# Seven-product pairs in half of the first quarter of layer 0's w1, with the input differences made during w_out

## The chip, the cores and the metric

The kernel runs on one core of one Trainium2 chip. The metric is the device time of one execution in microseconds (us). An execution is one launch that computes both layers for one sequence of 528 positions (16 meta tokens and 512 tokens).

## The reference: what is computed

The reference is a decoder trunk of two layers, all in float32. The part that matters here is the channel mixer, which follows the token mixer in each layer:

```python
def sq_relu_mlp(h, w1, w2):
    return jnp.square(jax.nn.relu(h @ w1.astype(h.dtype))) @ w2.astype(h.dtype)
...
        h = h + mix                       # mix ends with "@ w_out" in layer 0
        h = h + sq_relu_mlp(rmsnorm(h, norm_mlp_g[layer]), mlp_w1[layer], mlp_w2[layer])
```

h has 528 rows of 1024, w1 is 1024 x 4096 and w2 is 4096 x 1024. The mixer of layer 0 ends with a product with w_out (2048 x 1024), whose result is added to h.

## The kernel before, in words

**Layout.** Activations lie transposed: 1024 features are eight tiles of 128 partitions, each with 528 columns (positions). h0 to h7 are the residual stream. Each float32 operand of a matmul is split in two parts, a rounded one (names that end in h or hi) and the rest (l or lo), and a product takes three matmuls: hi·xh, hi·xl and lo·xh. One matmul is 128 x 128 weights by 264 columns.

**A plain product** (`gemm`) makes one tile of 128 output features for all 528 columns: 8 input tiles x 3 terms x 2 halves = 48 matmuls into the PSUM tile `mm`, of which there are two in turn. `prepare` makes the weights two products ahead: the load `raw`, ScalarE's cast to `whi`, and the subtraction for `wlo`, which is done on GpSimd for w_in and w_out and on VectorE for w1 and w2. There are three `whi` and three `wlo` buffers.

**A pair** is two output tiles made together by seven products instead of eight (Strassen-Winograd): the weights of both tiles are halved by input features (two loads `pr` of 512 KB), and the columns are halved too. Each of the seven products, A11, A12, S2, S3, S1, A22 and S4, is 4 input tiles x 3 terms = 12 matmuls into a PSUM tile `pp`, of which there are four in turn. S1 to S4 are sums of weight quarters (L231, VectorE, tiles `S`). Their splits are a cast on ScalarE (L246) and a subtraction on VectorE (L247). Nearly every product is read from PSUM by VectorE (`add` in `product`, L1037), which forms the rows `r` from them; A11 is copied by ScalarE to `snap` (L1039). `finish` applies the relu and the norm (L1021), and `squares` makes the next operand (ScalarE twice, then VectorE, L979). The next pair's S1 needs that pair's second `pr`, whose buffer comes free when the last use of an earlier one is done; there are three.

**The input's differences** (`differences(k)`, k = 0 to 3) are the column-half combinations that S1, S2 and S3 multiply with: two scaled copies and three casts on ScalarE, and seven VectorE instructions (L955 to L958, three of L963). S4's operand is written over half of x by `difference4`, during the last plain product.

**Order of the work.** w_out is done in two parts of eight products each. In the second (`residual`), each product is added to h by VectorE (L491), split to `x1h` and `x1l` (L420, L421), and its square is summed on GpSimd (`n1s`, L435). Then the PSUM pools are closed and opened anew, so that the first product of w1 takes the bank of w_out's last and waits for the addition to h7. In the MLP, the first 1024 hidden features (the first quarter, c = 0) are made by eight plain products, whose results wait for the norm `m0rb`; the differences are made during products 1 to 4. Then quarters 1 to 3 are made by four pairs each, and between them (`back`, after every second unit of two products) come the eight plain products of w2 for the quarter before. Layer 1 does the same with 512 columns.

**What sets the order.** From w_out on, TensorE, VectorE, ScalarE and GpSimd run their instructions in the order in which the code issues them (`manual_schedule`), except for a short stretch at w1's start, which a scheduler orders. Each engine works in order. Loads are issued by SyncE's queue, in order; a load waits until its buffer is free.

Of the kernel before, what the change touches and what calls it, by code (L numbers as in the profile page):

```python
# [17 lines left out]
P = 128  # L18
SEQ = 512
NMETA = 16  # L20
T = SEQ + NMETA
HT = T // 2
D = 1024
NK = D // P
# [105 lines left out]
H = NK // 2  # L130


PRODUCTS = [(kind, i) for i in range(NPAIR) for kind in ("A11", "A12", "S2", "S3", "S1", "A22", "S4")]


def mlp_units(layer):

    units = [(f"w1_{layer}", 0, m * P) for m in range(NK)]
    for c in range(1, 4):
        w2 = [(f"w2_{layer}", (c - 1) * D, m * P) for m in range(NK)]  # L140
        for j in range(len(PRODUCTS) // 2):
            units.append((f"s_{layer}", c, j))
            if j % 2:
                units.append(w2.pop(0))
        units += w2
    return units + [(f"w2_{layer}", 3 * D, m * P) for m in range(NK)]


def blocks():

    out = []
    for name, r, c in unit_order():
        if name[:2] != "s_":
            out.append((name, r, c))
        elif c == 0:
            out += [(f"w1_{name[2:]}", 0, r * D + m * P) for m in range(NK)]
    return out


@with_exitstack  # L160
def trunk(ctx, tc, xT, wts, par, con, out):
# [7 lines left out]
    def psums(n):  # L169
        st = ExitStack()  # L170
        return (st, st.enter_context(tc.tile_pool(name="pmm", bufs=2, space=PSUM, reuse_waits="tile")),
                st.enter_context(tc.tile_pool(name="pax", bufs=n, space=PSUM, reuse_waits="tile")))

    psum, pmm, pax = psums(2)
# [31 lines left out]
    class Pairs:  # L206

        def __init__(self, layer, pl):
            self.layer, self.pl = layer, pl
            self.todo = [(c, m) for c in range(1, 4) for m in range(NK)]  # L210
            self.raw, self.sums, self.used = {}, {}, {}
            self.live = 0

# [50 lines left out]
    def piece():  # L264
        if pieces:
            pieces.pop(0)()
# [120 lines left out]
    def gemm(what, x, n, at=NK, each=None):  # L387

        w = weights(what)
        ps = pmm.tile([P, 2, 512], F32, tag="mm", name=f"mm{state['unit']}")  # L390
        width = HT if n == T else SEQ
        halves = [(slice(i * width, i * width + width), ps[:, i, :width]) for i in range(n // width)]
        for k in range(NK):
            if k == at:
                between.chain_up()
            products(halves, w, k, x[k], k == 0, k == NK - 1)
            if each:
                each(k)
            if k % 2:
                between.step()  # L400
                piece()
        return ps[:, :, :HT] if n == T else ps[:, 0, :SEQ]

    def v2(ap, n):
        return two(ap) if n == T else ap
# [49 lines left out]
    def square(src, n, name):  # L455
        sq = sp.tile([P, T], F32, tag="sq", name=name)
        nc.scalar.activation(sq[:, :n], src, AF.Square)
        return sq[:, :n]
# [24 lines left out]
            return rb, xv  # L483
        return rb

    def residual(what, x, n, norm=None, xset=None, name="", keep=True):

        s = Sum(name, n) if norm is not None else None
        for m in range(NK):
            ps = gemm(what, x, n)  # L490
            nc.vector.tensor_tensor(v2(h[m][:, :n], n), ps, v2(h[m][:, :n], n), ALU.add)  # L491
            if norm is not None:
                split_g(xset[m], h[m][:, :n], col(PC_NORM + norm * NK + m), n)
                s.add(square(h[m][:, :n], n, f"{name}q{m}"))
        return s


    poolA = ExitStack()
    actA = poolA.enter_context(tc.tile_pool(name="actA", bufs=1, reuse_waits="tile"))
# [10 lines left out]
    engines = {nc.tensor.engine, nc.vector.engine, nc.scalar.engine, nc.gpsimd.engine}  # L510
# [28 lines left out]
    s = Sum("n0", T, nc.vector)  # L539
# [374 lines left out]
    setC = free[1]  # L914

    setD = new_set(act, "B", "x1")
    s = residual("w_out", setC, T, 2, setD, "n1")
    manual.close()
    mix.close()

    NQ, MW = 4, 32


    def mlp(layer, x, s, n, mine, after):
        hw = n // 2
        first, second = slice(0, hw), slice(hw, n)
        g = lambda k: col(PC_NORM + (2 + layer) * NK + k)
        with tc.tile_pool(name=f"mlp{layer}", bufs=1, reuse_waits="tile") as pl:
            hid = {}
            work = Pairs(layer, pl)  # L930
# [35 lines left out]
            def difference4(k):  # L966

                hi, lo = (t[:, second] for t in x[k])
                nc.scalar.activation(hi, t4[k], AF.Copy, scale=-1.0)
                nc.vector.scalar_tensor_tensor(lo, t4[k], -1.0, hi.bitcast(F32), ALU.mult, ALU.subtract)  # L970
# [8 lines left out]
                return lambda: nc.vector.tensor_tensor(dst[1][:, :n], q, dst[0][:, :n].bitcast(F32), ALU.subtract)  # L979

            what = f"w1_{layer}"
            ps = gemm(what, x, n)
            rb = rstd(s, f"m{layer}")
            work.load()
            manual = ExitStack()
            for m in range(NK):
                if m:

                    ps = gemm(what, x, n, each=(lambda k: k < H or difference4(k - H)) if m == NK - 1 else None)
                if m in (1, 2, 3, 4):  # L990
                    differences(len(t4))
                r = row(f"0{m}")
                nc.vector.scalar_tensor_tensor(v2(r, n), ps, 0.0, v2(rb[:, :n], n), ALU.max, ALU.mult)
                squares(hidden(0, m), r, f"0{m}")()
                if m == 0:
                    manual.enter_context(tc.manual_schedule(engines=engines))
# [16 lines left out]
                    e[1]()  # L1013

            stt = nc.vector.scalar_tensor_tensor
            for c in range(1, 4):
                rows = {}

                def finish(i, e, op):
                    r = rows[e]  # L1020
                    stt(r, r, 0.0, rb[:, :n], op, ALU.mult)  # L1021
                    m, c_ = 2 * i + e, c

                    def square():
                        low = squares(hidden(c_, m), r, f"{c_}{m}")
                        later(1, low)
                    later(2, square)

                def product(kind, i, w, half):
                    src, k0, sl = moving[kind]  # L1030
                    ps = pax.tile([P, 512], F32, tag="ax", name=f"pp{layer}{c}{i}{kind}")[:, :hw]
                    for k in range(H):
                        hi, lo = w[0][:, half * H + k, :], w[1][:, half * H + k, :]
                        xh, xl = (t[:, sl] for t in src[k0 + k])
                        for t, (l, rr) in enumerate(((hi, xh), (hi, xl), (lo, xh))):
                            nc.tensor.matmul(ps, l, rr, start=k == 0 and t == 0, stop=k == H - 1 and t == 2)  # L1036
                    add = lambda dst, y: nc.vector.tensor_tensor(dst, ps, y, ALU.add)  # L1037
                    if kind == "A11":
                        nc.scalar.copy(p1, ps)  # L1039
                    elif kind == "A12":  # L1040
                        rows[0] = row(f"{c}{i}0")
                        add(rows[0][:, first], p1)
                    elif kind == "S2":
                        add(u2, p1)
                    elif kind == "S3":
                        add(u3, u2)
                    elif kind == "S1":
                        rows[1] = row(f"{c}{i}1")
                        add(rows[0][:, second], u2)
                        add(rows[1][:, second], u3)  # L1050
                    elif kind == "A22":
                        add(rows[1][:, first], u3)
                        finish(i, 1, ALU.min)
                    elif kind == "S4":
                        add(rows[0][:, second], rows[0][:, second])
                        finish(i, 0, ALU.max)
                    tick()

                def back(m):
                    ps = gemm(f"w2_{layer}", hid[c - 1], n, each=lambda k: tick() if k % 2 else None)  # L1060
                    nc.vector.tensor_tensor(v2(h[m][:, :n], n), ps, v2(h[m][:, :n], n), ALU.add)  # L1061

                for j in range(len(PRODUCTS) // 2):
                    w = weights(f"s_{layer}")
                    for half in range(2):
                        product(*PRODUCTS[2 * j + half], w, half)
                    if j % 2:
                        back(j // 2)
                back(NK - 1)
            while queue:  # L1070
                tick()
            manual.close()
# [6 lines left out]
        setE = new_set(act, "B", "x2")  # L1079
        return residual("w2_0", x, T, 1, setE, "n2")  # L1080

    psum.close()
    psum, pmm, pax = psums(4)
    s = mlp(0, setD, s, T, (actA, "A"), after0)


    poolA.close()
# [337 lines left out]
    actA = poolA.enter_context(tc.tile_pool(name="actA", bufs=1, reuse_waits="tile"))  # L1425
    setF = new_set(actA, "A", "x3", SEQ)
    s = Sum("n3", SEQ)
# [9 lines left out]
    psum, pmm, pax = psums(4)  # L1437
# [87 lines left out]
```

## Time and profile before

| | |
|---|---|
| three runs | 1370.06, 1372.17 and 1372.92 us, median 1372.17 |
| the profiled execution | 1370.74 us, its span 1368.9 us |
| TensorE (PE), matmuls | 1351.0 us busy, 99% of the span |
| weight loads (PEld) | 1262.3 us, 92% |
| VectorE (DVE) | 1052.8 us, 77% |
| ScalarE (ACT) | 692.3 us, 51% |
| GpSimd (POOL) | 364.3 us, 27% |
| granted TensorE clock | 0.999 |

The second part of w_out lies at 335 to 381.5 us of the span, the eight plain products of w1's first quarter at 382.6 to 430.7, and the pairs from 430.7 on. A row of the timeline gives an instruction's start, its duration, engine, source line and tiles, and in brackets how long the engine had been idle ahead of it, and for whom. SPq is the queue of loads.

### The profile page before, as it was taken

How to read it: one execution, taken by the hardware profiler on the slowest of the kernel's cores; microseconds unless marked ns; L12 is line 12 of the kernel's file. 1: busy time of each engine (PE TensorE's matmuls, PEld its weight loads, DVE VectorE, ACT ScalarE, POOL GpSimd, SP SyncE). 2: the span in 40 equal slices, each digit the busy share in tenths (PEclk: the TensorE clock that was granted, in tenths of full speed). 3: DMA queues.
4: the chain of work that ended last, by engine and by line, in shares of the span. 5: the costliest groups of instructions: out<-in, count | busy, mean ns of one | idle time of the engine just before them, and what ended most of it. 6: DMA issues, size and time to landing. Idle time of an engine off the chain costs nothing. (4 is left out here: it accounts for less than half of the span.)

```text
span 1368.9 us, 24464 instructions
## 1 busy us (share of the span) xinstructions
PE 1351.0 (99%) x9673; PEld 1262.3 (92%) x9673; DVE 1052.8 (77%) x1847; ACT 692.3 (51%) x1353; POOL 364.3 (27%) x413
## 2 busy tenths in 40 slices
PE   8999999999999999999999999999999999999998
PEld 7999999999999999999999899998877898988987
DVE  5998899977367776777745799999987877777752
ACT  6434545467455443434432688888556443443420
POOL 2656554456600000000016434345640000000000
PEclk9999999999999999999999999999999999999999
DMA  5322221223322333232222444443342233233232
GB/s 193 107 94 78 64 76 63 64 79 105 126 91 78 91 110 95 91 109 78 78 94 85 132 125 114 119 109 93 94 139 84 87 105 111 79 122 105 66 108 77
DMA packets 39794, 134.08 MB, mean 98 GB/s; under 512 B 4992, under 2 KB 5120, under 8 KB 39680
## 3 DMA queue, kind: packets, MB, share of 16 engines
q1 hardware_dynamic: 39680, 132.52, 31.2%
q8 instruction: 76, 1.25, 0.4%
q14 instruction: 38, 0.31, 0.1%
HBM read 117.69 MB, written 2.10 MB: 88 GB/s over the span
## 5 line engine op out<-in xcount | busy, mean ns | idle before, releaser
L295 POOL TENSOR_TENSOR wlo<-raw,whi 128x256 fp32r<-128x256 f32 (+1 forms) x334 | 287.4, 880 | 267.6 <-ACT whi L292 133.1
L292 ACT CAST whi<-raw 128x256 fp32r<-128x256 f32 (+2 forms) x293 | 162.5, 590 | 208.5 <-PE mm L383 122.9
L623 DVE SCALAR_TENSOR_TENSOR acc<-cx,ptm,acc 128x526 f32<-128x526 f32 (+28 forms) x232 | 157.7, 742 | 3.5 <-ACT cx L618 3.5
L383 PE MATMUL mm<-xnh,whi 128*128 128x264 f32 x640 | 134.5, 292 | 3.0 <-DVE gt L711 2.3
L383 PE MATMUL mm<-xnl,whi 128*128 128x264 f32 x640 | 129.7, 284 | 0.7 <-DVE xnl L737 0.3
L383 PE MATMUL mm<-xnh,wlo 128*128 128x264 f32 x640 | 129.9, 284 | 0.0
L295 DVE TENSOR_TENSOR wlo<-raw,whi 128x1024 fp32r<-128x1024 f32 (+1 forms) x88 | 106.5, 1211 | 20.0 <-ACT whi L292 19.2
L383 PEld LDWEIGHTS mm<-xnh,whi 128*128 128x128 f32 x640 | 100.1, 189 | 6.5 <-issue 3.8
L383 PEld LDWEIGHTS mm<-xnl,whi 128*128 128x128 f32 x640 | 98.9, 188 | 1.6 <-DVE xnl L737 1.0
L383 PEld LDWEIGHTS mm<-xnh,wlo 128*128 128x128 f32 x640 | 98.8, 188 | 0.1
L247 DVE TENSOR_TENSOR wlo<-S,whi 128x512 fp32r<-128x512 f32 x96 | 65.1, 689 | 31.1 <-ACT whi L246 30.0
L435 POOL TENSOR_TENSOR n2s<-n2q,n2q 128x528 f32<-128x528 f32 x1 | 1.8, 1810 | 321.5 <-DVE wlo L295 321.5
L246 ACT CAST whi<-S 128x512 fp32r<-128x512 f32 x96 | 58.0, 617 | 55.4 <-DVE S L231 25.9
L383 PE MATMUL qk<-x2h,whi 128*128 128x264 f32 (+1 forms) x320 | 83.0, 323 | 0.5 <-ACT kraw L1191 0.5
L1061 DVE TENSOR_TENSOR h<-mm,h 128x528 f32<-128x528 f32 (+1 forms) x48 | 33.6, 699 | 62.2 <-PE mm L383 62.0
L383 PE MATMUL qk<-x2h,wlo 128*128 128x264 f32 (+1 forms) x320 | 77.3, 307 | 0.0
L383 PE MATMUL qk<-x2l,whi 128*128 128x264 f32 (+1 forms) x320 | 77.1, 306 | 0.0
L246 ACT CAST whi<-pr 128x512 fp32r<-128x512 f32 x72 | 43.4, 619 | 45.1 <-issue 10.3
L1326 DVE TENSOR_TENSOR_SCAN E<-kp,oz 128x527 f32<-128x527 f32 (+1 forms) x64 | 60.7, 968 | 3.7 <-ACT kp L1298 2.9
L383 PEld LDWEIGHTS qk<-x2h,whi 128*128 128x128 f32 x320 | 53.0, 190 | 2.7 <-ACT kraw L1191 0.9
L383 PEld LDWEIGHTS qk<-x2h,wlo 128*128 128x128 f32 x320 | 51.7, 188 | 2.9
L383 PEld LDWEIGHTS qk<-x2l,whi 128*128 128x128 f32 x320 | 51.7, 188 | 1.0
(1357 smaller groups left out, 4204.9 us busy)
## 6 DMA issues: line engine op xcount, KB each, us to landing
raw<-wts SPq DMA_DIRECT2D x168, 512.0 KB, 3.5
pr<-wts SPq DMA_DIRECT2D x48, 512.0 KB, 4.1
Q<-qhl SPq DMA_DIRECT2D x32, 256.0 KB, 5.1
K<-khl SPq DMA_DIRECT2D x32, 132.0 KB, 3.9
h<-xT SPq DMA_DIRECT2D x8, 264.0 KB, 5.4
out<-h SPq DMA_DIRECT2D x8, 256.0 KB, 2.0
raw<-wts SPq DMA_DIRECT2D x4, 256.0 KB, 5.3
ctm<-con SPq DMA_DIRECT2D x1, 790.0 KB, 6.7
```

The costliest lines, as they stand in the source:

```text
L246: nc.scalar.copy(hi[:, ks], src)
L247: nc.vector.tensor_tensor(lo[:, ks], src, hi[:, ks].bitcast(F32), ALU.subtract)
L292: (nc.scalar.copy if u == 0 and i else copy)(hi[:, ks], raw[:, ks])
L295: eng.tensor_tensor(lo[:, ks], raw[:, ks], hi[:, ks].bitcast(F32), ALU.subtract)
L383: nc.tensor.matmul(p, a[:, k, :], b[:, sl], start=(first and t == 0), stop=(last and t == 2))
L435: self.eng.tensor_tensor(new[:, :self.n], self.acc, src, ALU.add)
L623: nc.vector.scalar_tensor_tensor(a, cxf[:, s:T], tap(j, s), a, ALU.mult, ALU.add)
L1061: nc.vector.tensor_tensor(v2(h[m][:, :n], n), ps, v2(h[m][:, :n], n), ALU.add)
L1326: nc.vector.tensor_tensor_scan(E[:, 1:n], kp[:, :n - 1], zero.to_broadcast([P, n - 1]), 1.0, ALU.mult, ALU.add)
```

## The change

Of the first quarter of layer 0's w1, tiles 0 to 3 stay plain products, and tiles 4 to 7 become two pairs of seven products. No w2 product stands between these, since no quarter is done yet. The differences are made behind the second part of w_out: `residual` calls `behind(m)` at the end of each output tile, and at m = 4 to 7 that issues `differences(m - 4)`. The first three `pr` loads are issued ahead of that part, and `difference4` runs during the fourth plain product. Layer 1 keeps eight plain products. The new code is eleven lines longer above `residual`, so its lines bear other numbers.

```diff
+PLAIN = (4, NK)
+
+
+def first_products(layer):
+    return range(len(PRODUCTS) * PLAIN[layer] // NK // 2, len(PRODUCTS) // 2)
+
+
 def mlp_units(layer):
 
-    units = [(f"w1_{layer}", 0, m * P) for m in range(NK)]
+    units = [(f"w1_{layer}", 0, m * P) for m in range(PLAIN[layer])]
+    units += [(f"s_{layer}", 0, j) for j in first_products(layer)]
...
-            self.todo = [(c, m) for c in range(1, 4) for m in range(NK)]
+            self.todo = [(c, m) for c in range(4) for m in range(0 if c else PLAIN[layer], NK)]
...
-    def residual(what, x, n, norm=None, xset=None, name="", keep=True):
+    def residual(what, x, n, norm=None, xset=None, name="", behind=None):
...
                 s.add(square(h[m][:, :n], n, f"{name}q{m}"))
+            if behind:
+                behind(m)
...
     setD = new_set(act, "B", "x1")
-    s = residual("w_out", setC, T, 2, setD, "n1")
     manual.close()
     mix.close()
 
+    def before0(behind):
+
+        nonlocal psum, pmm, pax
+        with tc.manual_schedule(engines=engines):
+            s = residual("w_out", setC, T, 2, setD, "n1", behind)
+        psum.close()
+        psum, pmm, pax = psums(4)
+        return s
...
             what = f"w1_{layer}"
+            if before:
+                work.load()
+                s = before(lambda m: m < H or differences(m - H))
             ps = gemm(what, x, n)
             rb = rstd(s, f"m{layer}")
-            work.load()
+            if not before:
+                work.load()
             manual = ExitStack()
-            for m in range(NK):
+            for m in range(PLAIN[layer]):
                 if m:
 
-                    ps = gemm(what, x, n, each=(lambda k: k < H or difference4(k - H)) if m == NK - 1 else None)
-                if m in (1, 2, 3, 4):
+                    ps = gemm(what, x, n, each=(lambda k: k < H or difference4(k - H)) if m == PLAIN[layer] - 1 else None)
+                if not before and m in (1, 2, 3, 4):
                     differences(len(t4))
...
-            for c in range(1, 4):
+            for c in range(4):
...
-                for j in range(len(PRODUCTS) // 2):
+                for j in range(len(PRODUCTS) // 2) if c else first_products(layer):
                     w = weights(f"s_{layer}")
                     for half in range(2):
                         product(*PRODUCTS[2 * j + half], w, half)
-                    if j % 2:
+                    if c and j % 2:
                         back(j // 2)
-                back(NK - 1)
+                if c:
+                    back(NK - 1)
```

Two places show how instructions move. The first is VectorE at the end of w_out. Before, between the additions of products 6 and 7 to h6 and h7 (the row of h6 and what follows it):

```order
L491 TENSOR_TENSOR h6_85<-mm57_4765,h6_85 128x528
L421 SCALAR_TENSOR_TENSOR x1l6_4350<-h6_85,pt_77,x1h6_4349 128x528
L295 TENSOR_TENSOR wlo57_4822<-raw57_4823,whi57_4821 128x1024
L491 TENSOR_TENSOR h7_86<-mm58_4827,h7_86 128x528
L295 TENSOR_TENSOR wlo58_4923<-raw58_4924,whi58_4922 128x1024
L421 SCALAR_TENSOR_TENSOR x1l7_4352<-h7_86,pt_77,x1h7_4351 128x528
```

And in the changed kernel, from the same row on:

```order
L502 TENSOR_TENSOR h6_85<-mm57_4833,h6_85 128x528
L432 SCALAR_TENSOR_TENSOR x1l6_4350<-h6_85,pt_77,x1h6_4349 128x528
L976 SCALAR_TENSOR_TENSOR t0l2_4890<-h2_81,pt_77,t0h2_4889 128x264
L977 SCALAR_TENSOR_TENSOR t0l2_4890<-t0l2_4890,t0h2_4889 128x264
L978 TENSOR_TENSOR t0h6_4891<-t0h2_4889 128x264
L979 SCALAR_TENSOR_TENSOR t0h6_4891<-h6_85,pt_77,t0l2_4890 128x264
L984 TENSOR_TENSOR T01l2_4364<-t0l2_4890,T01h2_4363 128x264
L984 TENSOR_TENSOR T02l2_4372<-t0l2_4890,T02h2_4371 128x264
L984 TENSOR_TENSOR T03l2_4380<-t0h6_4891,T03h2_4379 128x264
L306 TENSOR_TENSOR wlo57_4905<-raw57_4906,whi57_4904 128x1024
L502 TENSOR_TENSOR h7_86<-mm58_4910,h7_86 128x528
```

Seven instructions of `differences` stand between `x1l` and `wlo`, and so ahead of the addition to h7, as they do ahead of those to h5 and h6.

The second place is VectorE at the head of the pairs. Before, it is that of quarter 1 (`pp010`, the first pair), from the splits for A22 to the next pair's first sums:

```order
L247 TENSOR_TENSOR wlo67_5559<-pr011_4992,whi67_5558 128x512
L231 TENSOR_TENSOR S4_010_5564<-pr010_4990,S2_010_5387 128x512
L1037 TENSOR_TENSOR snap0_5521<-pp010S2_5570,snap0_5521 128x264
L1037 TENSOR_TENSOR snapu0_5522<-pp010S3_5584,snap0_5521 128x264
L247 TENSOR_TENSOR wlo68_5599<-S4_010_5564,whi68_5598 128x512
L247 TENSOR_TENSOR wlo68_5599<-pr012_4994,whi68_5598 128x512
L231 TENSOR_TENSOR S1_011_5604<-pr013_5566 128x512
L231 TENSOR_TENSOR S2_011_5606<-pr012_4994,S1_011_5604 128x512
L1061 TENSOR_TENSOR h0_79<-mm69_5608,h0_79 128x528
```

In the changed kernel it is that of quarter 0 (`pp002`, tiles 4 and 5; then `pp003`):

```order
L258 TENSOR_TENSOR wlo62_5275<-pr005_4385,whi62_5274 128x512
L242 TENSOR_TENSOR S4_002_5280<-pr004_4383,S2_002_5138 128x512
L1062 TENSOR_TENSOR r0020_5313<-pp002A12_5300,snap0_5272 128x264
L258 TENSOR_TENSOR wlo63_5316<-S4_002_5280,whi63_5315 128x512
L258 TENSOR_TENSOR wlo63_5316<-pr006_4387,whi63_5315 128x512
L242 TENSOR_TENSOR S1_003_5321<-pr007_5282 128x512
L242 TENSOR_TENSOR S2_003_5323<-pr006_4387,S1_003_5321 128x512
L1062 TENSOR_TENSOR snap0_5272<-pp002S2_5325,snap0_5272 128x264
L1062 TENSOR_TENSOR snapu0_5273<-pp002S3_5339,snap0_5272 128x264
L258 TENSOR_TENSOR wlo64_5354<-pr006_4387,whi64_5353 128x512
```

The first sum of the next pair, which reads the fourth load `pr007`, stands here ahead of the additions that read S2 and S3 from PSUM (`snap`, `snapu`); before, it stood behind them, and a w2 product (`h0`) followed.

More of the change, by code (lines that the diff above doesn't have):

```diff
@@ L154, in blocks @@
             out.append((name, r, c))
-        elif c == 0:
+        elif r and c == 0:
             out += [(f"w1_{name[2:]}", 0, r * D + m * P) for m in range(NK)]
+        elif not r and c == first_products(int(name[2:]))[0]:
+            out += [(f"w1_{name[2:]}", 0, m * P) for m in range(PLAIN[int(name[2:])], NK)]
     return out
@@ L916, in trunk, with mlp @@
     setD = new_set(act, "B", "x1")
-    s = residual("w_out", setC, T, 2, setD, "n1")
     manual.close()
     mix.close()
+    def before0(behind):
[5 more added lines that the diff above has]
+        return s
     NQ, MW = 4, 32
-    def mlp(layer, x, s, n, mine, after):
+    def mlp(layer, x, s, n, mine, after, before=None):
         hw = n // 2
@@ L1080, in after0 @@
         return residual("w2_0", x, T, 1, setE, "n2")
-    psum.close()
-    psum, pmm, pax = psums(4)
-    s = mlp(0, setD, s, T, (actA, "A"), after0)
+    s = mlp(0, setD, None, T, (actA, "A"), after0, before0)
     poolA.close()
```

## Prediction, made before the changed kernel was run

> **What bounds the kernel now.** I read the page first, then the waits of TensorE, then timelines of the two stretches that the change rebuilds.
>
> ```profile
> span 1368.9 us, 24464 instructions
> PE 1351.0 (99%) x9673; PEld 1262.3 (92%) x9673; DVE 1052.8 (77%) x1847; ACT 692.3 (51%) x1353; POOL 364.3 (27%) x413
> PE mm L383 <- ACT whi L292: 0.9, 1, 0.9
> PE mm L383 <- DVE r L993: 0.6, 1, 0.6
> ```
>
> TensorE is busy 99% of the span; the last two rows are all that it waits from 300 to 460 us (total, times, longest). So time goes by the matmuls that are left, as long as VectorE, at 77%, keeps pace. Whether it does is a question of the stage. The end of w_out:
>
> ```profile
> 370.14 0.71 DVE L491 TENSOR_TENSOR h<-mm,h 128x528 f32<-128x528 f32 x1 [3.51 <-PE mm L383]
> 371.53 0.64 ACT L457 ACTIVATE n1q<-h 128x528 f32<-128x528 f32 x1
> 371.66 0.77 DVE L421 SCALAR_TENSOR_TENSOR x1l<-h,pt,x1h 128x528 fp32r<-128x528 f32 x1 [0.81 <-ACT x1h L420]
> 372.06 1.03 ACT L292 CAST whi<-raw 128x1024 fp32r<-128x1024 f32 x1
> 372.59 1.33 POOL L435 TENSOR_TENSOR n1s<-n1s,n1q 128x528 f32<-128x528 f32 x1 [1.95 <-ACT n1q L457]
> 373.18 1.82 DVE L295 TENSOR_TENSOR wlo<-raw,whi 128x1024 fp32r<-128x1024 f32 x1 [0.76 <-ACT whi L292]
> 375.93 0.71 DVE L491 TENSOR_TENSOR h<-mm,h 128x528 f32<-128x528 f32 x1 [0.93 <-PE mm L383]
> 381.71 0.71 DVE L491 TENSOR_TENSOR h<-mm,h 128x528 f32<-128x528 f32 x1 [1.19 <-PE mm L383]
> 382.56 0.48 PE L383 MATMUL mm<-x1h,whi 128*128 128x264 f32 x2 [0.89 <-ACT whi L292]
> ```
>
> Additions to h come every 5.78 us (375.93 to 381.71), one product of 48 matmuls: 0.1205 us each. The last row is w1's first product. The profile names a cast, but that whi was cast a product earlier; what ends just ahead of it is the addition to h7 (381.71 + 0.71 = 382.42), for whose bank it waits. Here VectorE has 0.93 to 1.19 us to spare in each product.
>
> The pairs of quarter 1, whose instructions are those that two pairs of quarter 0 will run:
>
> ```profile
> L1036 PE MATMUL pp010A<-x1h,whi x12: 283/283/287, 430.7 to 445.0; 128*128 128x264 f32 x12
> 432.08 0.70 DVE L993 SCALAR_TENSOR_TENSOR r<-mm,m0rb 128x528 f32<-128x528 f32 x1
> 434.04 0.71 DVE L979 TENSOR_TENSOR hid00l<-q,hid00h 128x528 fp32r<-128x528 f32 x1 [1.25 <-ACT q L978]
> 437.06 0.69 DVE L247 TENSOR_TENSOR wlo<-pr,whi 128x512 fp32r<-128x512 f32 x1
> 437.78 0.93 SPq L218 DMA_DIRECT2D pr<-wts  x2
> 442.14 0.69 DVE L231 TENSOR_TENSOR S<-pr 128x512 f32<-128x512 f32 x1 [1.71 <-DMA pr<-wts]
> 442.86 0.69 DVE L231 TENSOR_TENSOR S<-pr,S 128x512 f32<-128x512 f32 x1
> 443.47 0.70 DVE L1061 TENSOR_TENSOR h<-mm,h 128x528 f32<-128x528 f32 x1
> 445.56 0.42 DVE L1037 TENSOR_TENSOR r<-pp010S,snapu 128x264 f32<-128x264 f32 x1
> 445.90 0.42 DVE L1037 TENSOR_TENSOR r<-pp010A,snapu 128x264 f32<-128x264 f32 x1
> 446.36 0.71 DVE L1021 SCALAR_TENSOR_TENSOR r<-r,m0rb 128x528 f32<-128x528 f32 x1
> 446.99 0.68 DVE L247 TENSOR_TENSOR wlo<-pr,whi 128x512 fp32r<-128x512 f32 x1
> 447.59 0.68 DVE L247 TENSOR_TENSOR wlo<-S,whi 128x512 fp32r<-128x512 f32 x1
> 449.88 0.70 DVE L979 TENSOR_TENSOR hid01l<-q,hid01h 128x528 fp32r<-128x528 f32 x1
> 451.72 1.29 DVE L247 TENSOR_TENSOR wlo<-S,whi 128x512 fp32r<-128x512 f32 x2 [1.14 <-ACT whi L246]
> ```
>
> Starts give the pitch of VectorE's work: a read of a product 0.34 us (445.56 to 445.90; 0.46 to one that needs its result, 446.36), L1021 0.63, a split 0.60, a sum of quarters 0.61 (442.86 to 443.47), L979 as L1021. A pair needs 7 splits, 4 sums, 7 reads, 2 of L1021 and 2 of L979: 4.2 + 2.4 + 2.4 + 1.3 + 1.3 and four dependences of 0.12 = 12.1 us. Its seven products take TensorE 7 x 12 x 0.1205 = 10.1. In quarters 1 to 3, w2 products of 5.78 us each lie between them, and TensorE doesn't feel that VectorE waited 1.71 us for a load here. In quarter 0 nothing lies between.
>
> **The change, part by part.**
>
> *Removed matmuls.* Two pairs of 84 instead of 96: 24 x 0.1205 = **-2.9 us**. The order of TensorE's instructions shows that these pairs are made by seven products.
>
> *Differences behind w_out.* Their own length, and what GpSimd does to VectorE:
>
> ```profile
> 399.04 1.23 DVE L295 TENSOR_TENSOR wlo<-raw,whi 128x1024 fp32r<-128x1024 f32 x1 [0.24 <-ACT whi L292]
> 399.33 0.50 ACT L953 ACTIVATE t0h<-h,pt 128x264 f32<-128x264 f32 x1
> 400.19 0.49 DVE L955 SCALAR_TENSOR_TENSOR t0l<-h,pt,t0h 128x264 f32<-128x264 f32 x1
> 402.56 0.43 DVE L963 TENSOR_TENSOR T03l<-t0h,T03h 128x264 fp32r<-128x264 f32 x1
> 326.21 2.01 POOL L295 TENSOR_TENSOR wlo<-raw,whi 128x256 fp32r<-128x256 f32 x2 [0.32 <-ACT whi L292]
> 326.39 1.24 DVE L695 TENSOR_TENSOR hdn<-hdn,lnrb 128x528 f32<-128x528 f32 x1
> 329.34 0.69 DVE L695 TENSOR_TENSOR hdn<-hdn,lnrb 128x528 f32<-128x528 f32 x1
> ```
>
> One set takes VectorE 2.80 us (400.19 to 402.99) once ScalarE's first copy is there. That copy takes the cast's place at 372.06 and lasts 0.50, so the set runs from 372.6 to 375.4, a free wlo (1.23) ends at 376.7, and the addition to h6 starts near 376.65 instead of 375.93: 0.7 late. The next set starts that much later and loses 0.7 again: h7 is 1.4 late, with nothing else wrong. For h5, with no wlo on VectorE, 0.5 us are left over. An h that is late stops nobody at h5 and h6 (two mm tiles in turn); at h7 it stops w1's first product, with all of TensorE behind it.
>
> That is the lower end. Each set also starts while GpSimd sums the square (n1s, 1.33 us), and the first runs into the w_out pieces on GpSimd too. VectorE under GpSimd's work is slower: 1.82 against 1.23 for wlo, 1.24 against 0.69 for the same instruction at 326.39 and 329.34. Three sets under n1s at 0.59, two meetings with pieces at 0.55, less the 0.5 to spare: +2.4. Bounds: 0 and 2.9 (each instruction held until GpSimd's ends). I take the measured prices: **+3.8 us** (1.4 to 4.3).
>
> [...]
>
> *The norm's chain.* The wait of 0.6 us for r goes: in the old order a set of differences stands amid the norm's instructions on VectorE, in the new one it doesn't. **-0.6** (-0.6 to 0).
>
> *The pairs without w2 between them.* Count from the first product, at 430.7 in the rows. The last plain r starts at +1.4 (432.08), its L979 at +3.3 and ends at +4.05; then the two splits of unit (S1, A22) end at +5.3, and with the last of them the buffer for the fourth load is free (before: 437.06 + 0.69, load at 437.78). It lands 442.14 - 437.78 = 4.36 later, at +9.65. VectorE has S4's sum, a read and two splits until then (0.6 + 0.34 + 1.2 from +5.3: +7.4) and waits 2.2 us, in order, with the sums S1 and S2 of the next pair ahead of the read of S2's product: that starts at +9.65 + 1.33 = +11.0. TensorE has four pp tiles: its seventh product needs S2's tile and arrives after six of 12 x 0.1205 = 1.446, at +8.7, so it stands 2.7 us.
>
> From that read on VectorE is behind and sets the pace. Up to the read of the second A22, which frees the tile for product 17, its order holds 11 reads (3.8), 10 splits (6.0), 5 sums (3.0), 2 of L1021 (1.3), 2 of L979 (1.2) and five dependences (0.6): 15.9 us. ScalarE's casts, behind the squares in its order, keep it waiting once or twice as at 451.72 (1.14): 1.9. So that read ends at 11.0 + 17.8 + 0.4 = +29.2, where TensorE alone would be there after 16 x 1.446 = +23.1: 6.1 late. The first w2 product then needs a wlo that stands behind all this: 0.8. **+6.9 us.** Lower end: without the load's wait and ScalarE's, 15.9 + 11.0 + 0.4 - 23.1 - 2.2 = 2.0. Upper end, by the slowest landing:
>
> ```profile
> DMA to landing us min/median/max: 4.3/5.0/6.8
> ```
>
> 6.8 - 4.4 = 2.4 more, 9.3.
>
> *At nothing.* The loads that now go out ahead of w_out's second part are as many as before; their buffers are free by then (before, the first goes out amid that part's first loads), and the casts that need the raw tiles behind them run two products, 11.6 us, ahead of use. Without that cover three loads of 4.4 us in a row could cost 13 - 11.6 = 1.6. The differences' old place only had VectorE idle. ScalarE, at 51%, counts through its casts above.
>
> Sum: -2.9 + 3.8 - 0.6 + 6.9 = **+7.2 us**; bounds -0.1 and +10.7 (-2.9 + 4.3 + 9.3). The profiled execution took 1370.74 us (span 1368.9 and 1.8 around it), 1.4 below the runs' median of 1372.17. With the three runs its mean is 1371.5. From there: **1378.7 us**.
>
> **Rivals.** *TensorE stays the bound* (5%): weights two products ahead and four pp tiles absorb what VectorE lacks, and h7's addition is no later than now. Then -2.9 - 0.6 = -3.5: 1368.0. For it: 99%, and the load's wait that cost nothing at 442. Against: there a product of 5.78 us lay behind it. It decides when VectorE needs less than 10.1 us per pair; the rows give 12.1. [...]
>
> *The small case* (11%): the fourth load lands before VectorE asks for it, ScalarE's casts are in time, and GpSimd's work disturbs nobody: -2.9 + 1.4 - 0.6 + 2.0 to 4.0 = -0.1 to +1.9, some 1372.5. For it: before, VectorE's wait there was 1.71, less than the 2.2 reckoned here. Against: the fastest landing above is 4.3.
>
> *The large case* (10%): the loads land late (6.8), and each set is held by GpSimd fully: -2.9 + 4.3 - 0.6 + 9.3 = +10.1, 1381.6.
>
> *The forecast* (74%): +3 to +9, that is 1374.5 to 1380.5.
>
> **The numbers.** 0.2% of 1371.5 is 2.7 us, about what this measurement can tell from no change. Faster 0.05 (first rival), same 0.11 (the small case), slower 0.84 (forecast and large case). The range leaves out the first rival and the ends of the others: 1372.3 to 1382.3.
>
> **What would show it.** Right: w1's first product waits 3 to 5 us for the addition to h7, with VectorE busy without a pause ahead of it; the wait for r is gone; in the pairs of quarter 0 TensorE stands three to five times for reads of pp tiles, 5 to 8 us in all, first for S2's, behind a wait of VectorE for pr; from the first w2 product on the same time as before. Wrong: no row of TensorE waiting for L1062 there, or VectorE idle within that stage while TensorE is not; the forecast falls if VectorE gets through both pairs in about 20 us.

## The result, and the profile after

The changed kernel takes 1377.92 us (median of five runs, 1377.35 to 1378.67). The kernel before took 1372.04 us beside it (1369.93 to 1372.92). The ratio is 1.0052, with a 95% interval of 1.0041 to 1.0063: slower by 5.9 us, where the forecast was 7.2 more than the kernel before and 1378.7 in all.

The page of the changed kernel, and then the waits of TensorE from 300 to 470 us (total, times, longest):

```profile
span 1375.6 us, 24471 instructions
PE 1350.7 (98%) x9649; PEld 1261.7 (92%) x9649; DVE 1069.9 (78%) x1879; ACT 697.3 (51%) x1365; POOL 365.0 (27%) x413
```

```profile
PE mm L394 <- DVE h L502: 5.1, 1, 5.1
PE pp002S L1061 <- DVE snap L1062: 1.3, 1, 1.3
PE pp003A L1061 <- DVE r L1062: 1.3, 1, 1.3
PE pp010A L1061 <- DVE snapu L1062: 0.7, 1, 0.7
PE mm L394 <- DVE wlo L306: 0.4, 1, 0.4
PE pp010S L1061 <- DVE r L1062: 0.4, 1, 0.4
```

The 24 matmuls are gone (9649 instead of 9673). The wait for r (0.6 before) is gone. In exchange w1's first product waits 5.1 us for the addition to h7 (0.9 before), and in the pairs TensorE stands four times for VectorE's reads, 3.7 us in all (2.6 in quarter 0's, 1.1 in quarter 1's first), and once for a wlo. On the page all of this is one point of TensorE's busy share, 98% instead of 99%.

**The end of w_out**, VectorE, GpSimd and the first matmul of w1 on the timeline:

```profile
378.04 0.70 DVE L502 TENSOR_TENSOR h<-mm,h 128x528 f32<-128x528 f32 x1
380.19 1.35 POOL L446 TENSOR_TENSOR n1s<-n1s,n1q 128x528 f32<-128x528 f32 x1 [5.97 <-ACT n1q L468]
380.49 1.34 DVE L976 SCALAR_TENSOR_TENSOR t0l<-h,pt,t0h 128x264 f32<-128x264 f32 x1 [0.17 <-ACT t0h L973]
385.34 0.70 DVE L502 TENSOR_TENSOR h<-mm,h 128x528 f32<-128x528 f32 x1
386.18 0.78 PE L394 MATMUL mm<-x1h,whi 128*128 128x264 f32 x2 [5.07 <-DVE h L502]
```

Two additions to h are 7.30 us apart here (378.04 to 385.34), where a product of w_out takes 5.78. Between them VectorE runs a whole set of differences. Its first instruction lasts 1.34 us, because GpSimd's sum n1s runs from 380.19 to 381.54; the same instruction took 0.49 in the kernel before (400.19), with nothing on GpSimd.

**The clock behind that pause.** The last column but two of this view is the granted clock, in windows of 1 us:

```profile
core 0: us, PE busy (x), PEclk, DMA share, GB/s
385.00:386.00 1.00, 0.00 (x0) 0.84 0.00 0
386.00:387.00 1.00, 0.82 (x4) 0.50 0.32 45
387.00:388.00 1.00, 1.00 (x6) 0.50 0.89 348
388.00:389.00 1.00, 1.00 (x7) 0.50 0.62 176
389.00:390.00 1.00, 1.00 (x9) 0.95 0.74 229
```

From the end of the pause until 389.1 TensorE runs at half its clock, 4 to 7 matmuls per us instead of the 9 of the next row. The first 14 matmuls take 3.09 us (386.18 to 389.27) instead of 14 x 0.1205 = 1.69. These 1.4 us are not in the prediction.

**The pairs of quarter 0**: the group of the first pair's A products, then of quarter 1's first pair (min/median/max in ns, first and last start), and the loads' queue, VectorE and TensorE on the timeline:

```profile
L1061 PE MATMUL pp002A<-x1h,whi x12: 282/283/288, 411.7 to 420.1; 128*128 128x264 f32 x12
L1061 PE MATMUL pp010A<-x1h,whi x12: 283/286/361, 436.1 to 451.8; 128*128 128x264 f32 x12
```

```profile
411.66 0.28 PE L1061 MATMUL pp002A<-x1h,whi 128*128 128x264 f32 x1
412.61 0.70 DVE L1018 SCALAR_TENSOR_TENSOR r<-mm,m0rb 128x528 f32<-128x528 f32 x1
416.50 0.93 SPq L229 DMA_DIRECT2D pr<-wts  x2
419.99 0.69 DVE L242 TENSOR_TENSOR S<-pr 128x512 f32<-128x512 f32 x1 [0.85 <-DMA pr<-wts]
421.33 0.42 DVE L1062 TENSOR_TENSOR snap<-pp002S,snap 128x264 f32<-128x264 f32 x1
421.90 0.36 PE L1061 MATMUL pp002S<-x1h,whi 128*128 128x264 f32 x1 [1.30 <-DVE snap L1062]
439.14 0.42 DVE L1062 TENSOR_TENSOR r<-pp003A,snapu 128x264 f32<-128x264 f32 x1
```

Fourteen products at 1.446 us would take 20.2 us; from 411.7 to 436.1 they took 24.4. VectorE waits 0.85 us for the fourth load, reads S2's product 9.7 us after the stage's start (421.33 - 411.66), and 17.8 us later reads the second A22's (439.14). In that stretch TensorE is the one that waits.

### The profile page after: what moved, and what is told of

The parts are those of the page before. It is cut to its first block, busy times and chain, and to the rows that moved or that the text cites. A ratio compares the mean times of both kernels' runs of the same rounds, so it can differ in the third digit from the quotient of the medians.

```text
span 1375.6 us, 24471 instructions
## 1 busy us (share of the span) xinstructions
PE 1350.7 (98%) x9649; PEld 1261.7 (92%) x9649; DVE 1069.9 (78%) x1879; ACT 697.3 (51%) x1365; POOL 365.0 (27%) x413
## 5 line engine op out<-in xcount | busy, mean ns | idle before, releaser
L303 ACT CAST whi<-raw 128x256 fp32r<-128x256 f32 (+2 forms) x289 | 158.2, 584 | 199.8 <-PE mm L394 114.7
L306 DVE TENSOR_TENSOR wlo<-raw,whi 128x1024 fp32r<-128x1024 f32 (+1 forms) x84 | 100.8, 1201 | 18.1 <-ACT whi L303 17.2
L257 ACT CAST whi<-S 128x512 fp32r<-128x512 f32 x104 | 62.8, 616 | 67.2 <-DVE S L242 37.4
L258 DVE TENSOR_TENSOR wlo<-S,whi 128x512 fp32r<-128x512 f32 x104 | 70.5, 688 | 32.4 <-ACT whi L257 31.3
L257 ACT CAST whi<-pr 128x512 fp32r<-128x512 f32 x78 | 46.9, 619 | 45.4 <-issue 10.3
L258 DVE TENSOR_TENSOR wlo<-pr,whi 128x512 fp32r<-128x512 f32 x78 | 53.4, 685 | 4.4 <-ACT whi L257 4.1
```

The source lines that it names most:

```text
L257: nc.scalar.copy(hi[:, ks], src)
L258: nc.vector.tensor_tensor(lo[:, ks], src, hi[:, ks].bitcast(F32), ALU.subtract)
L303: (nc.scalar.copy if u == 0 and i else copy)(hi[:, ks], raw[:, ks])
L306: eng.tensor_tensor(lo[:, ks], raw[:, ks], hi[:, ks].bitcast(F32), ALU.subtract)
```

## The experiments

**How they are read.** The text of the program ahead of w_out's second part is the same in all these kernels, and yet that part starts between 334.2 and 337.9 us in ten traces: near 30 us some executions show half clock or one more wait of 1.4 to 2.2 us that others don't, and near 960 us half clock lasts 6.8 us in no_lo and splits_gpsimd and 3.4 in the other eight. A difference of 1 us between medians is therefore not told apart by a handful of runs, but a difference of stages in a trace is. The table gives, from the group rows of the traces, when six places of the program are reached: the start of w_out's second part, of w1, of quarter 0's pairs, of quarter 1's pairs, of the first w2 product of hidden quarter 0 and of hidden quarter 1. The last column but one is the time from the first place to the last, less the 188.8 us of the kernel before (524.0 - 335.2).

| kernel | w_out, 2nd part | w1 | pairs, q0 | pairs, q1 | w2, q0 | w2, q1 | stage against before | median, ratio to before (95%) |
|---|---|---|---|---|---|---|---|---|
| before | 335.2 | 382.6 | - | 430.7 | 436.6 | 524.0 | 0 | |
| changed | 334.7 | 386.2 | 411.7 | 436.1 | 442.7 | 530.8 | +7.3 | 1377.92, 1.0052 (1.0041 to 1.0063) |
| diffs_alone | 334.2 | 385.5 | - | 435.1 | 441.0 | 528.4 | +5.4 | 1375.87, 1.0035 (1.0022 to 1.0049) |
| pairs_alone | 336.0 | 383.3 | 408.3 | 437.6 | 444.2 | 532.3 | +7.5 | 1379.06, 1.0054 (1.0041 to 1.0066) |
| no_sums | 335.9 | 384.5 | 410.2 | 434.6 | 441.3 | 529.3 | +4.6 | 1374.35, 1.0026 (1.0015 to 1.0036) |
| busy_wait | 335.8 | 387.2 | 411.4 | 435.9 | 442.5 | 530.6 | +6.0 | 1376.66, 1.0041 (1.0028 to 1.0055) |
| load_early | 335.7 | 387.2 | 412.8 | 436.3 | 442.9 | 531.0 | +6.5 | 1379.54, 1.0061 (1.0045 to 1.0076) |
| no_lo | 337.7 | 389.2 | 415.1 | 435.6 | 441.5 | 528.9 | +2.4 | 1374.62, 1.0026 (1.0016 to 1.0035) |
| splits_gpsimd | 336.4 | 387.8 | 414.0 | 440.5 | 447.1 | 535.2 | +10.0 | 1382.18, 1.0080 (1.0066 to 1.0094) |
| interleaved | 337.9 | 385.3 | 397.9 | 434.0 | 440.6 | 528.7 | +2.0 | 1374.53, 1.0018 (1.0010 to 1.0027) |

In interleaved, plain products 2 and 3 lie within the stretch from 397.9 to 434.0. The kernel before had a median of 1371.12 us beside diffs_alone to busy_wait, and of 1371.15 beside the four others.

### The differences behind w_out alone: diffs_alone

```diff
-PLAIN = (4, NK)
+PLAIN = (NK, NK)
```

> The differences stay behind w_out, but the first quarter is eight plain products again (no pairs there, no 24 matmuls saved). Theory (the addition to h7 is late and TensorE then runs at half clock for some 3 us): w1's first product waits 5 us for the addition, against 0.9 before (+4.2), then some 14 matmuls run at a granted clock of 0.5 (+1.4), and the wait of 0.6 for r is gone: +5.0 us against the kernel before, 1.0036. Rival (the loss belongs to the pairs, the differences move into idle time): within 1 us of the kernel before.

The first quarter is eight plain products again, and the kernel is still slower, by 1.0035. w1 starts 51.3 us after w_out's second part instead of 47.4, and the eight plain products then take 49.6 us (385.5 to 435.1) instead of 48.1, though the wait for r is gone. The granted clock says why (windows of 2 us, the columns as above):

```profile
386.00:388.00 2.00, 2.00 (x11) 0.50 0.60 229
390.00:392.00 2.00, 2.00 (x16) 0.86 0.09 35
```

It is 0.50 from 383.75 to 390.6, some 5 us of w1's work, where the changed kernel has 3. So moving the differences costs 5.4 us in this trace: 3.9 by the later addition to h7 and 1.5 net of the clock's loss and r's gain.

### The pairs alone: pairs_alone

```diff
-                s = before(lambda m: m < H or differences(m - H))
+                s = before(None)
...
-                if not before and m in (1, 2, 3, 4):
+                for _ in range((1, 1, 2, 0)[m] if before else m in (1, 2, 3, 4)):
                     differences(len(t4))
```

> The two pairs of quarter 0 stay, but the differences are made during the plain products of w1 (one set during the first and second, two during the third). Theory (VectorE can't keep pace with pairs that have no w2 product between them): w1's first product waits 0.9 us as before, the clock stays at full speed, -2.9 us for the matmuls, and in the pairs TensorE stands at least the 4 to 5 us that it stands in the changed kernel, more because two sets now lie just ahead of the first pair: +2 to +8 us against the kernel before. Rival (only the move of the differences costs, the pairs are a gain): -2.9 us, 0.998.

The differences are back in the plain products, of which there are only four. w1 starts in time (47.3 us) and at full clock, and yet the kernel is as slow as the changed one. All of it is lost from the pairs on, which take 29.3 us (408.3 to 437.6) instead of 20.2:

```profile
413.99 0.70 DVE L1018 SCALAR_TENSOR_TENSOR r<-mm,m0rb 128x528 f32<-128x528 f32 x1
417.25 0.46 PE L1061 MATMUL pp002S<-T01h,whi 128*128 128x264 f32 x1 [2.91 <-ACT snap L1064]
422.80 0.43 DVE L1062 TENSOR_TENSOR snap<-pp002S,snap 128x264 f32<-128x264 f32 x1
423.38 0.36 PE L1061 MATMUL pp002S<-x1h,whi 128*128 128x264 f32 x1 [1.39 <-DVE snap L1062]
440.62 0.43 DVE L1062 TENSOR_TENSOR r<-pp003A,snapu 128x264 f32<-128x264 f32 x1
```

```profile
418.00:420.00 2.00, 2.00 (x11) 0.50 0.52 92
```

VectorE comes out of the differences late: the last plain r is read 5.7 us into the stage (413.99 - 408.34) instead of 0.95, and S2's product 14.5 us into it instead of 9.7. From there to the second A22 it takes 17.82 us again, just what the changed kernel takes. The clock, expected to stay at full speed, is 0.50 from 417.4 to 420.8 (the last row, a window of 2 us), behind the pause of 2.91 us. That adds nothing here: VectorE waits for no product ahead of S2's read, TensorE stands another 1.39 us for that read, and the pairs take 4.9 us longer than in the changed kernel because the read comes 4.8 later. So the two halves of the change don't add up: alone they cost 5.4 and 7.5, together 7.3, since the first half takes VectorE's work out of the stage in which the second half is short of VectorE.

### What GpSimd's sums add: no_sums

```diff
-                s.add(square(h[m][:, :n], n, f"{name}q{m}"))
+                q = square(h[m][:, :n], n, f"{name}q{m}")
+                if not behind or m == NK - 1:
+                    s.add(q)
```

> The changed kernel without the seven additions of the squares on GpSimd behind w_out (the norm of layer 0's MLP then sees the last square only; that part of the computation is left out). Theory (each set of differences starts while GpSimd adds a square and is held by it): the first instruction of a set takes 0.49 us instead of 1.3 to 1.6, the addition to h7 comes 2 to 2.8 us sooner, w1's first product waits 2.3 to 3 us instead of 5.1. If the half clock needs a longer pause than that, it is gone too: 3.5 to 4.2 us less than the changed kernel's +5.9, else 2 to 2.8 less. Rival (the differences' own length makes h7 late): less than 0.7 us sooner.

The wait for h7 falls from 5.1 to 2.2 us. The first instruction of the set, in the same place as the one of 1.34 us above:

```profile
379.74 0.49 DVE L978 SCALAR_TENSOR_TENSOR t0l<-h,pt,t0h 128x264 f32<-128x264 f32 x1 [0.18 <-ACT t0h L975]
384.55 0.48 PE L394 MATMUL mm<-x1h,whi 128*128 128x264 f32 x2 [2.18 <-DVE h L502]
```

What is left above the 0.89 of before, 1.29 us, is the sets' own length (1.4 in the prediction); the other 2.9 us are GpSimd's sums (2.4 in the prediction). This kernel shows half clock as well, from 385.2 to 388.6, after a pause of only 2.2 us.

### The same wait without the pause: busy_wait

```diff
+        if fill:
+            pd = pax.tile([P, 512], F32, tag="ax", name="fill")
+            for _ in range(fill):
+                nc.tensor.matmul(pd[:, :HT], w[0][:, 0, :], x[0][0][:, :HT], start=True, stop=True)
...
-            ps = gemm(what, x, n)
+            ps = gemm(what, x, n, fill=34 if before else 0)
```

> The changed kernel with 34 matmuls of 264 columns (4.1 us, into a PSUM tile that nothing reads) on TensorE ahead of w1's first product, where it waits some 5 us anyway. Theory (the half clock follows from the pause): the granted clock stays at 1.0, w1's first fourteen matmuls take 1.7 us instead of 3.1, and the kernel is 1.4 us faster than the changed one (+4.5 against the kernel before). Rival (the slow stretch has another cause, the three loads or the start of a new stage): the same slow stretch, no gain, or 0.1 to 0.5 lost.

Thirty-four matmuls whose result nobody uses fill the wait for h7. w1 starts no earlier (51.4 us after w_out's second part, 51.5 in the changed kernel), but its four plain products take 24.2 us (387.2 to 411.4) instead of 25.5, and the clock doesn't fall:

```profile
388.00:390.00 2.00, 2.00 (x19) 1.00 0.72 248
```

So the half clock is what the pause brings, and costs 1.3 us here, as the 1.4 counted from the changed kernel's matmuls. The median moves by as much (1376.66 against 1377.92), though the intervals of the two ratios overlap.

### The fourth load ahead of time: load_early

```diff
+        def extra(self):
+            t = wp.tile([P, NK, P], F32, tag="raw", name=f"px{self.layer}", bufs=2)
+            nc.sync.dma_start(t, wts[place[f"w1_{self.layer}", 0, (NK - 1) * P]])
+            self.raw[0, NK - 1] = t
...
+                if before and m == 1:
+                    work.extra()
```

> The changed kernel with the fourth load of quarter 0's pairs put in a buffer of the plain loads, issued during the second plain product instead of at the end of a split of the first pair. Theory (the load's wait is the smaller part, VectorE's rate the larger): VectorE's wait of 0.85 us for that load is gone, TensorE's first stop shrinks from 1.3 us to about 0.4, the later ones stay: 0.9 us less than the changed kernel. Rival (the load starts the delay of all that follows): the stops shrink by 3 us or more.

The weights of the last tile go into a `raw` buffer; the load goes out at 388.25, 32 us before VectorE reads it. Its wait of 0.85 us is gone, and TensorE's first stop falls from 1.30 to 0.35:

```profile
420.21 0.68 DVE L247 TENSOR_TENSOR S<-px 128x512 f32<-128x512 f32 x1
421.54 0.42 DVE L1069 TENSOR_TENSOR snap<-pp002S,snap 128x264 f32<-128x264 f32 x1
422.11 0.36 PE L1068 MATMUL pp002S<-x1h,whi 128*128 128x264 f32 x1 [0.35 <-DVE snap L1069]
439.36 0.43 DVE L1069 TENSOR_TENSOR r<-pp003A,snapu 128x264 f32<-128x264 f32 x1
```

S2's read comes 8.7 us into the stage instead of 9.7, the second A22's again 17.82 us after it, and the pairs take 23.5 us instead of 24.4. The load is worth 0.9 us of the stage and no more; the rest is VectorE's own work. The median of the runs doesn't show this gain: at 1379.54 it lies 1.6 us above the changed kernel's, with intervals that overlap. Only one of these executions was traced, and in it the stage is 0.8 us shorter; what the others lost, and where, stays open.

### Less work for VectorE: no_lo

```diff
-                nc.vector.tensor_tensor(lo[:, ks], src, hi[:, ks].bitcast(F32), ALU.subtract)
+                if c:
+                    nc.vector.tensor_tensor(lo[:, ks], src, hi[:, ks].bitcast(F32), ALU.subtract)
...
-                        hi, lo = w[0][:, half * H + k, :], w[1][:, half * H + k, :]
+                        hi, lo = w[0][:, half * H + k, :], w[1 if c else 0][:, half * H + k, :]
```

> The changed kernel without the 14 subtractions (wlo) for the pairs of quarter 0; the third term multiplies the rounded part again, so TensorE does the same matmuls (the low parts of these weights are left out). VectorE has 14 x 0.6 = 8.4 us less in that stage, nothing else changes. Theory (VectorE's rate sets the pace in these pairs): of the 4 to 5 us that TensorE stands there, at most 1 is left (the first, behind the load): 3.5 to 4.5 us less than the changed kernel, so +1.4 to +2.4 against the kernel before. Rival (the load of the fourth weight tile or the PSUM tiles themselves): less than 1 us gained.

With VectorE's splits for quarter 0's pairs left out, the matmuls being as many, every stop behind w1's first product is gone. The only wait of TensorE from 300 to 620 us, and VectorE's reads:

```profile
PE mm L395 <- DVE h L503: 5.0, 1, 5.0
```

```profile
421.85 0.69 DVE L242 TENSOR_TENSOR S<-pr 128x512 f32<-128x512 f32 x1 [2.83 <-DMA pr<-wts]
423.19 0.42 DVE L1063 TENSOR_TENSOR snap<-pp002S,snap 128x264 f32<-128x264 f32 x1
437.14 0.43 DVE L1063 TENSOR_TENSOR r<-pp003A,snapu 128x264 f32<-128x264 f32 x1
```

From S2's read to the second A22's it is 13.95 us instead of 17.8, and the pairs take 20.5 (415.1 to 435.6), 0.3 more than TensorE's own 20.2. VectorE even waits 2.83 us for the load, longer than in any other kernel, and TensorE doesn't stand for it. The stage is 4.9 us shorter than in the changed kernel, although the same pause is there and half clock behind it lasts longer, 6.8 us (386.3 to 393.1) instead of 3.4. By the medians less is gained: +3.5 us against the kernel before, where +1.4 to +2.4 was expected. The traced execution has more half clock than the changed kernel's near 30 us (3.4 us, against none) and near 960. The pair stage is bound by VectorE's work, and the load only shows where that work leaves no slack.

### The splits on GpSimd: splits_gpsimd

```diff
-                nc.vector.tensor_tensor(lo[:, ks], src, hi[:, ks].bitcast(F32), ALU.subtract)
+                (nc.vector if c or q else nc.gpsimd).tensor_tensor(lo[:, ks], src, hi[:, ks].bitcast(F32), ALU.subtract)
```

> The changed kernel with seven of the 14 subtractions for quarter 0's pairs (the first of each unit) on GpSimd, which is idle there. [...] Theory: about 1 us less than the changed kernel. If GpSimd's work disturbs nobody: 3 us less. If it holds VectorE fully: no gain, or a loss of up to 3.

One of the two splits of each unit goes to GpSimd, which is idle there. A gain of about 1 us was the author's estimate (a loss of up to 3 if GpSimd held VectorE fully), and the stage became 2.7 us longer. VectorE and GpSimd at one place, and TensorE's first stop:

```profile
410.95 1.31 POOL L258 TENSOR_TENSOR wlo<-S,whi 128x512 fp32r<-128x512 f32 x1 [4.47 <-ACT whi L257]
411.02 1.79 DVE L242 TENSOR_TENSOR S<-pr,pr 128x512 f32<-128x512 f32 x1
425.98 0.37 PE L1061 MATMUL pp002S<-x1h,whi 128*128 128x264 f32 x1 [3.02 <-DVE snap L1062]
```

GpSimd takes 1.31 us for a split that costs VectorE 0.69, and VectorE's next instruction, which starts 0.07 us later, lasts 1.79 instead of 0.69 and ends after GpSimd's (412.26). S2's read moves to 11.4 us into the stage, and the second A22's follows 18.1 us later (17.8 in the changed kernel, with all its splits on VectorE). So the pairs take 26.5 us instead of 24.4: work given to GpSimd is not taken from VectorE here. The other part of the 2.7 us is the clock: behind the pause ahead of w1 it is 0.50 for 6.8 us (385.4 to 392.2) instead of 3.4, and the plain products take 26.2 us instead of 25.5. It is 0.50 again behind the stop of 3.02 us, from 426.35 to 429.8, which costs the pairs nothing: they wait for VectorE's reads, and VectorE waits for no product there.

### Plain products between the pairs' products: interleaved

```diff
+FIRST = (0, 1, 7, 2, 8, 3, 9, 10, 11, 12, 13)
+SETS = {4: (0,), 7: (1, 2)}
...
-                s = before(lambda m: m < H or differences(m - H))
+                s = before(lambda m: [differences(k) for k in SETS.get(m, ())])
...
-                for j in range(len(PRODUCTS) // 2) if c else first_products(layer):
+                for j in range(len(PRODUCTS) // 2) if c else FIRST[LEAD:] if before else ():
+                    if c == 0 and j < PLAIN[layer]:
+                        ps = gemm(what, x, n, each=(lambda k: k < H or difference4(k - H)) if j == 3 else None)
...
+                        plain(j, ps)
+                        continue
```

> Both losses attacked at once: one set of differences behind w_out's fifth product, two behind its last, one in w1's second product; and the order of quarter 0 is plain, plain, unit 1, plain, unit 2, plain, units 3 to 7, so that three plain products cover the head of the pairs. Theory (VectorE has 12.1 us of work for a pair's 10.1, and cover helps only where it stands): w1's first product waits 0.9 us, the clock stays, and TensorE still stands 3 to 6 us behind the last plain product, where five units and the next quarter's first two follow without cover: 0 to +3.5 us against the kernel before. Rival (the order was the fault, and with cover the saved matmuls show): -2 to -3 us.

Only one set of differences stands ahead of the addition to h7, and plain products 2 and 3 stand between units of the first pair, so that VectorE has time there. The waits of TensorE from 300 to 470 us:

```profile
PE pp003A L1069 <- ACT whi L262: 1.5, 1, 1.5
PE pp003A L1069 <- DVE r L1070: 1.3, 1, 1.3
PE mm L399 <- DVE h L507: 0.9, 1, 0.9
PE pp010A L1069 <- DVE snapu L1070: 0.7, 1, 0.7
PE mm L399 <- DVE wlo L311: 0.4, 1, 0.4
PE pp010S L1069 <- DVE r L1070: 0.4, 1, 0.4
```

The wait for h7 is that of the kernel before (0.9), the clock stays at 1.00 there, and S2's product waits for nothing. The stage is 5.3 us shorter than in the changed kernel. But five stops of 4.3 us remain in the second pair and behind it, more than the 2.9 us that the removed matmuls bring: with a ratio of 1.0018 (1.0010 to 1.0027) it is better than the change and not as good as the kernel before. None of the kernels run beats that one.

## Why the prediction was right, and where its terms were off

The time was 1377.92 us against 1378.7, within the range, and slower as forecast. Against the kernel run beside it that is +5.9 us, where +7.2 was forecast. The two traced executions differ by 6.7 us (spans 1375.6 and 1368.9): +7.3 in the stage, -0.5 ahead of it; what else parts them from the medians is not shown. The terms, measured in the trace of the changed kernel by the stages of the table:

| step of the prediction | predicted | measured |
|---|---|---|
| Removed matmuls | -2.9 | -2.9 (9673 - 9649 = 24) |
| Differences behind w_out | +3.8 (1.4 to 4.3) | +4.2 (h7's wait 5.07 - 0.89) |
| The norm's chain | -0.6 | -0.6, r's wait gone |
| The pairs without w2 between them | +6.9 (2.0 to 9.3) | +5.6 (24.4 - 20.2, then 0.7 behind pp010A and 0.7 behind w2's first product) |
| not in it: the half clock | 0 | +1.4 |
| sum | +7.2 | +7.7 by these rows, +7.3 by the stage's ends |

**Differences behind w_out.** The mechanism held with both of its shares: 1.29 us for the sets' own length (1.4) and 2.9 for GpSimd (2.4). The first instruction of each of the four sets ends 0.29 us after GpSimd's sum does (380.49 + 1.34 = 381.83; 380.19 + 1.35 = 381.54) and lasts 1.34 to 1.57 us, where it took 0.49 in the kernel before (400.19), so VectorE was held to the end, which was the upper end of this term, 4.3. The price of 0.59 that the sum used was too low: here it is 0.85 (1.34 - 0.49) or more. splits_gpsimd shows VectorE held at another place, 1.79 us instead of 0.69, with its end 0.55 us after GpSimd's (412.81 against 412.26).

**The step that was missed.** The prediction priced the pause ahead of w1 at its length alone. The clock behind it is no term of the sum, nor among what the prediction put "at nothing". Behind the pause TensorE ran at half clock until 389.1, and busy_wait showed that the pause is the cause: filled with matmuls, it left the clock at 1.00 and gave back 1.3 us. The trace of the kernel before had this to show: there TensorE pauses for 3.14 us ahead of 955.61, and its granted clock is 0.57 from 955 to 957 and 0.58 from 957 to 959.

**The pairs.** The prediction had S2's read at +11.0 and then 17.8 us of VectorE's work to the second A22's read. The 17.8 was measured exactly (421.33 to 439.14; in pairs_alone and load_early 17.82), and no_lo shows that VectorE's work is what it consists of. In part this exactness is luck: the 1.9 us in it for ScalarE's casts stood for "once or twice" 1.14, and the two waits were 1.14 and 0.69. The mis-sized number is the first: S2's read came at +9.7, since the fourth load went out at +4.8 instead of +5.3 and landed in 3.5 us instead of 4.4, so that VectorE waited 0.85 us and not 2.2. That wait was worth 0.9 us of the stage (load_early). This and the missing clock term, 1.3 and 1.4 us with opposite signs, nearly cancelled: by luck the sum was nearer than its parts.

**What was to show it.** The wait for h7 was 5.07 us (3 to 5 said), VectorE ahead of it without a pause from 380.49 on; r's wait gone; four stops for pp tiles, first S2's and behind VectorE's wait for pr, as said, but 3.7 us in all, below the 5 to 8 said, and 1.1 of it in quarter 1's first pair. The time was as before not from the first w2 product on, behind which 0.7 us more was lost, but from hidden quarter 1's: 844.9 us to the end of the span before, 844.8 here.

**The rivals.** TensorE does not stay the bound: the two pairs took 24.4 us and not 20.2. The small case wanted the load early and GpSimd out of the way; load_early and no_sums made these two conditions one at a time, and each alone left the stage 6.5 and 4.6 us longer than before; both together were not run. Of the large case one condition came true, sets held fully by GpSimd; the loads as late as 6.8 us did not occur.

## What to carry to other kernels

An algorithm that saves matmuls is paid for on the engine that prepares and combines them. The occupancy of that engine over the whole program (77% here) doesn't say whether it can pay; its work per block against the matmuls' time per block, in the stage where nothing else lies between, does (12.1 us against 10.1). Work that is moved ahead of a critical hand-over should be priced with the engines that are busy at its new place, and a pause of the matmul engine with the clock that follows it: here half clock came behind pauses of 2.18 us (no_sums) to 5.07 (the changed kernel).

## What the runs showed of the hardware that was not expected

**Half clock after a pause.** All five kernels that waited about 5 us at w1's start (the changed one, diffs_alone, no_lo, load_early, splits_gpsimd; 4.85 to 5.07 us) show a granted clock of 0.50 behind it, for 3.4 us in all (385.7 to 389.1, load_early the same length) or 6.8 (diffs_alone, 383.8 to 390.6, no_lo and splits_gpsimd the same length). The lengths are one and two times 3.4 us. The clock fell also behind shorter pauses: 2.18 us (no_sums), 2.91 (pairs_alone) and 3.02 (splits_gpsimd).

Which pauses brought it can be read from the traces. In those of the kernel before and of the changed one, all changes of the clock lie whole multiples of 3.413 us apart (in the changed kernel the falls at 385.69 and 962.54 lie 169 of them apart), so each can be cut into windows of that length. In the five windows at full clock ahead of a fall TensorE stood still for 2.80 to 3.41 us (the window's length less TensorE's busy time): 3.41 us ahead of 385.69 and 3.11 ahead of 962.54 in the changed kernel, 2.80 ahead of 955.27 in the kernel before, and 3.41 and 2.95 at the ends of these traces. In all their other whole windows at full clock it stood for 1.72 or less, and the clock stayed. Half clock ended after one window where TensorE stood for 0.49 us of it (from 385.69), 0.00 (from 962.54) and 0.34 (from 955.27). In diffs_alone, no_lo and splits_gpsimd w1's first product started 1.8, 2.9 and 2.4 us after the fall, and half clock lasted for two windows. A pause of 2.29 us near 27 us shows both outcomes, in the changed kernel and then in diffs_alone (window, its length, busy time of TensorE and matmuls, granted clock, DMA share and GB/s):

```profile
23.88:27.29 3.41, 1.69 (x14) 1.00 0.37 105
27.29:30.70 3.41, 2.84 (x23) 1.00 0.12 49
25.35:28.76 3.41, 1.12 (x10) 1.00 0.48 145
28.76:32.17 3.41, 3.41 (x17) 0.50 0.00 0
```

In the changed kernel the end of a window divides the pause, 1.72 and 0.57 us, and the clock stays; in diffs_alone the pause falls into one window whole, and the clock falls behind it. So in these traces the place of a pause in the windows, which differs from trace to trace, goes with its cost: nothing or 3.4 us of half clock for this one, 3.4 or 6.8 us for one of about 5. Since the clock fell behind a pause of 2.18 us (no_sums), the standstill that brings it begins, by these windows, between 1.72 and 2.18 us; where is not shown.

**A free GpSimd is not free help.** A subtraction on GpSimd took 1.31 us and lengthened the VectorE instruction that it met from 0.69 to 1.79, so that with seven splits moved away from VectorE the pairs took 2.1 us longer.
